# Half of an MLP's up projections by seven half-size products in place of eight, on one Trainium2 core

## The chip, the cores and the metric

The kernel runs on one core of one Trainium2 chip. The core has a matrix engine (TensorE, PE in the profile; its weight loads are PEld), a vector engine (VectorE, DVE), a scalar engine (ScalarE, ACT), GpSimd (POOL) and SyncE (SP), whose queue issues nearly all DMA transfers here. The metric is the device time of one execution in microseconds, as the median of several runs.

## The reference

The program is a decoder trunk of two layers over 256 tokens of width 2048, in float32. Layer 0 uses differential attention, layer 1 latent attention; each layer then attends into 256 memory tokens and ends in a squared-ReLU MLP with 8192 hidden columns.

```python
def sq_relu_mlp(h, wup, wdown):
    return jnp.square(jax.nn.relu(h @ wup)) @ wdown

def reference(...):
    mem_h = rms_norm(mem, mem_norm)
    for i in range(DEPTH):                   
        h = rms_norm(x, attn_norm[i])
        x = x + (diff_attention if i % 2 == 0 else mla_attention)(h, ...)
        x = x + memory_cross_attention(rms_norm(x, cross_norm[i]), mem_h, ...)
        x = x + sq_relu_mlp(rms_norm(x, mlp_norm[i]), mlp_wup[i], mlp_wdown[i])
    return rms_norm(x, final_norm)
```

wup is 2048 x 8192, wdown 8192 x 2048. The MLP is the largest part: two products of 256 x 2048 x 8192 in each layer.

## The kernel before

**Arithmetic.** Every product of float32 matrices is made of three TensorE passes. Each operand is split into a high part (a cast to the matrix format) and a low part (the rest), and high x high, high x low and low x high are added up in PSUM.

**Weights.** A weight matrix is stored as units of 512 rows of K by 512 columns, 1 MB each, laid out as 128 partitions x 2048. `split_weights` (L173) loads one into a `raw` buffer (4 of them, `RAWS`), and for each half of it ScalarE casts the high part `whi` (L187) and VectorE subtracts to get `wlo` (L188). `whi` and `wlo` have four half-size buffers each (`whalf`), so TensorE's halves of the current unit and the next one fill them. `plan` is the list of all units in order of use; `fill` (L195) keeps `AHEAD` = 3 of them issued ahead, and `take` (L203) hands over the next one. Loads stand in program order on SP's queue.

**Matmuls.** `matmul_chunk` (L212) makes 256 x 512 outputs in two PSUM banks, one per tile of 128 tokens (t = 0, 1). A unit of weights gives 2 halves x 2 token tiles x 2 pieces of K x 3 passes = 24 matmuls of 128x128 by 128x512. All matmuls are recorded at L155, all transposes (128x128, also on TensorE) at L159.

**Order.** TensorE's instructions run in the order in which the program writes them. The other engines' order is set by a scheduler at build time. To place transposes among matmuls, the program keeps a clock of its own (`clock`): work that follows a chunk is a `Task`, a generator that yields how many microseconds its next step should be put off, and `pump` (L113), called after every part of a unit, runs the steps that are due. `need` (L120) forces the tasks that a matmul depends on. The constants `T_SQ` = 4.4, `T_TURN` = 2.6, `T_ADD` = 2.2 are such put-offs. Nothing checks them against the chip: where a step is placed too early, TensorE stands until its input is there.

**The MLP** (`mlp`, L808) has four blocks of 2048 hidden columns. `up` (L813) makes four chunks of 512 columns, each from 4 units; per token tile, ScalarE takes relu and the row's scale out of PSUM (L821), GpSimd squares (L822), TensorE transposes four times, and `split` (L268) makes the high and low parts of the hidden columns as the stationary operand of the next product. `down` makes four chunks of the output from the block's four hidden tiles and adds each to the residual rows `x` (L349). The order is up 0, down 0, up 1, and so on.

**Around it.** `Stream.feed` (L329) turns the residual rows after the last projection into the transposed, split operand of the next layer part. PSUM has eight banks, four for matmul chunks (`ps_mm`) and four for everything else (`ps_ax`). The attention parts use tiles `ev`, `xg`, `p` and `pT` of the pool `work`; `mem_norm` (L719) loads the memory rows into `xg` tiles; `tables` (L686) makes the rotary tables, from constants and positions that are loaded by hooks at the first six units.

Of the kernel before, what the change touches and what calls it, by code (L numbers as in the profile page):

```python
# [23 lines left out]
WARM = 16  # L24
RAWS = 4
MLP_BLOCKS = 4

# [16 lines left out]
def trunk(ctx, tc, x, xT, mem, memT, positions, gcols, gfinal, lam_vecs, consts, W, out):  # L44
# [24 lines left out]
    def half_unit():  # L69
        return units.tile([P, 2, 2, S], F32R, tag="half", name=nm("half"), bufs=3)  # L70

    def bank(tag="ax"):
        p = ps_mm if tag == "mm" else ps_ax
        return p.tile([P, CH], F32, tag=tag, name=nm(tag))

# [51 lines left out]
    class Held:  # L127
# [6 lines left out]
        def run(self, gen):  # L134
            self.tasks.append(Task(gen))
            return self

        def __getitem__(self, i):
            return self.tile[i]
# [21 lines left out]
    def f32(ap):  # L161
        return ap.bitcast(F32)
# [10 lines left out]
    def split_weights(src, width, pieces=2, loads=1, queue=None):  # L173
        raw = raw_tile()
        n = 4 * width
        m = n // loads
        for i in range(loads):
            load(raw[:, i * m : (i + 1) * m], src[:, i * m : (i + 1) * m], queue)
        m = n // pieces
        halves = []  # L180
        for i in range(pieces):
            at = i * m % (n // 2)
            if at == 0:
                halves.append([whalf.tile([P, 2 * CH], F32R, tag=tag, name=nm(tag)) for tag in ("whi", "wlo")])
            hi, lo = (w[:, at : at + m] for w in halves[-1])
            r = raw[:, i * m : (i + 1) * m]
            nc.scalar.copy(hi, r)  # L187
            nc.vector.tensor_tensor(lo, r, f32(hi), ALU.subtract)  # L188
        return halves

    plan = []
    ready = []
    AHEAD = 3

    def fill():  # L195
        while len(ready) < AHEAD and plan:
            name, i, width = plan.pop(0)
            ready.append(split_weights(W[name][i, :, : 4 * width], width))

# [3 lines left out]
    def take():  # L203
# [6 lines left out]
        return got  # L210

    def matmul_chunk(acts, width=CH, turns=False):  # L212

# [3 lines left out]
        def part(u, h, hi, lo, t):  # L217
            o = ps[t][:, :width]
            a = acts[u]
            for k in range(2):  # L220
                kk = 2 * h + k
                first = u == 0 and kk == 0
                last = u == n - 1 and kk == 3
                ah = a[:, 0, kk, t * P : (t + 1) * P]
                al = a[:, 1, kk, t * P : (t + 1) * P]
                wh = hi[:, k * width : (k + 1) * width]
                wl = lo[:, k * width : (k + 1) * width]
                mmul(o, ah, wh, first, False)
                mmul(o, ah, wl, False, False)
                mmul(o, al, wh, False, last)  # L230
            pump()

# [22 lines left out]

    const = keep.tile([P, NC_], F32, name="const")
    g = keep.tile([P, NG], F32, name="g")
    pos = keep.tile([P, NT], I32, name="pos")
    lamv = work.tile([P, 4, P], F32, tag="ev", name="lamv", bufs=6)
    xs = [keep.tile([P, D], F32, name=f"x{t}") for t in range(NT)]  # L260
    ident = const[:, C_ID : C_ID + P]
    identr = keep.tile([P, P], F32R, name="identr")
    maskr = keep.tile([P, P], F32R, name="maskr")
    mhalf = keep.tile([P, 1], F32, name="mhalf")
# [10 lines left out]
    def scaled(src, cols):  # L275
        tmp = work.tile([P, 4, P], F32, tag="xg", name=nm("xg"))
        nc.vector.tensor_tensor(tmp, src, cols.unsqueeze(2).broadcast_to([P, 4, P]), ALU.mult)  # L277
        return tmp
# [42 lines left out]
    class Stream:  # L321


        def __init__(self, gcol):
            self.gcol = gcol
            self.units = {}
            self.ss = [small.tile([P, 4], F32, tag="ss", name=nm("ss")) for _ in range(NT)]

# [14 lines left out]
        def done(self):  # L343
            self.rstd = [row_norm(self.ss[t], D)[:, 0:1] for t in range(NT)]
            return [self.units[c] for c in range(4)]

    def add_residual(t, c, ps):
        xc = xs[t][:, c * CH : (c + 1) * CH]
        nc.vector.tensor_tensor(xc, xc, ps, ALU.add)  # L349


    def evacuate(ps, scale):
        e = work.tile([P, CH], F32, tag="ev", name=nm("ev"), bufs=6)
        nc.scalar.activation(e[:, : ps.shape[1]], ps, AF.Copy, scale=scale)  # L354
        return e
# [47 lines left out]
    def softmax(sb, n):  # L403
# [3 lines left out]
        ssum = small.tile([P, 4], F32, tag="ssum", name=nm("ssum"))  # L407
        pr = work.tile([P, CH], F32, tag="p", name=nm("p"), bufs=3)
        nc.vector.tensor_reduce(nmax[:, :n], sb.rearrange("p (n k) -> p n k", n=n), AX.X, ALU.max, negate=True)  # L409
# [9 lines left out]
    def prob_T(src, n, pt):  # L419

        for i in range(n):
            flip(pt[:, i * P : (i + 1) * P], src[:, i * P : (i + 1) * P])
        o = work.tile([P, 2, CH], F32R, tag="pT", name=nm("pT"), padded_shape=[P, 2, 4 * S])
# [102 lines left out]
    def attend_diff(q, k, v, dst, coef, subcols):  # L526
# [33 lines left out]
        def normed(t, blocks, out):  # L560
# [6 lines left out]
            r = rsqrt_mean(ss, 2, S)  # L567
            os = work.tile([P, CH], F32, tag="p", name=nm("os"), bufs=3)
            nc.vector.tensor_tensor(
# [43 lines left out]
    def plan_mlp(l):  # L613
        for b in range(MLP_BLOCKS):
            plan_k(f"mlp_wup{l}", 16, start=16 * b)
            plan_k(f"mlp_wdown{l}", 16, start=16 * b)

# [68 lines left out]
    def tables():  # L686
# [26 lines left out]
        for i in range(2):  # L713
            nc.vector.tensor_scalar(gsub[:, 2 * i : 2 * i + 2], g[:, G_SUB : G_SUB + 2], 1.0 - LAMBDA_INIT, None, ALU.mult)
        nc.scalar.copy(identr, ident)
        nc.scalar.copy(maskr, const[:, C_MASK : C_MASK + P])
    mem_rstd = []

    def mem_norm():  # L719
        for t in range(NT):  # L720
            ss = small.tile([P, 4], F32, tag="ss", name=nm("ss"))
            for c in range(4):
                mt = work.tile([P, CH], F32, tag="xg", name=nm("memrow"), padded_shape=[P, 4 * P])
# [29 lines left out]
    def project_out(acts_o, gcol):  # L753
        nxt = Stream(gcol)
        for c in range(4):
# [52 lines left out]
    def mlp(l, norm, gnext):  # L808
# [3 lines left out]

        def up(b):  # L813
            hid[b] = []
            for c in range(4):
                dst = Held(unit())
                ps = matmul_chunk(a)

                def task(t, ps, dst):
                    r = work.tile([P, CH], F32, tag="ev", name=nm("ev"), bufs=6)  # L820
                    nc.scalar.activation(r, ps, AF.Relu, scale=rstd[t])  # L821
                    nc.gpsimd.tensor_tensor(r, r, r, ALU.mult)  # L822
                    yield T_SQ
                    split(dst, t, transpose4(r, ps))
                    yield T_TURN

                for t in range(NT):
                    dst.run(task(t, ps[t], dst))
                hid[b].append(dst)

        def down(b, nxt=None):
            for c in range(4):
                ps = matmul_chunk(hid[b], turns=nxt is not None and c == 3)
                for t in range(NT):
                    add_residual(t, c, ps[t])
                    if nxt is not None:
                        nxt(c, t, ps[t])

        for b in range(MLP_BLOCKS):
            up(b)  # L840
            if b < MLP_BLOCKS - 1:
                down(b)
        if gnext is None:
            return down
        nxt = Stream(gnext)
        down(b, nxt.feed)
        return nxt

# [37 lines left out]
    hm = MLA_ROPE // 2  # L886
    krope = Held(half_unit())
    LAT = 3 * P
# [23 lines left out]
    def latent_rows():  # L912
        return [work.tile([P, CH], F32, tag="ev", name=nm("lat"), bufs=6) for _ in range(NT)]

# [11 lines left out]
    for t in range(NT):  # L926
        e = work.tile([P, 2, P], F32, tag="kr", name=nm("kr"))
        nc.vector.memset(e, 0.0)
# [72 lines left out]
    load(gf, gfinal)  # L1001
    ss = [small.tile([P, 4], F32, tag="ss", name=nm("ss")) for _ in range(NT)]

# [17 lines left out]

    down(MLP_BLOCKS - 1, finish)

# [86 lines left out]
```

## Time and profile before

| what | value |
|---|---|
| median of 3 runs | 2323.3 us (2322.37 to 2324.17) |
| profiled execution, its own time | 2322.5 us |
| span of its instructions | 2320.8 us |
| mean granted TensorE clock | 0.997 |
| MLP of layer 0 / layer 1, about | 543 to 1230 us / 1629 to 2310 us |
| DMA | 425.36 MB, 183 GB/s over the span |
| matmuls at L155, mean recorded duration | 9504 of chunks, 387 to 389 ns (neighbours overlap) |
| one 1 MB weight load, issue to landing | 5.0 us |
| GpSimd's square (L822), x64 | 1272 ns |
| ScalarE's relu (L821), x64 | 685 ns |

Matmuls overlap in the records, so their rate is read from a stretch: its length by the number of matmuls in it. An "idle before" column says how long an engine stood ahead of a group, and behind the arrow what ended it.

### The profile page before, as it was taken

The page shows a single profiled execution, that of the slowest core. Times are in us where ns is not written, and L with a number is a line of the kernel's source. Part 1 is how long each engine was busy: PE and PEld are TensorE (multiplying, and loading weights), DVE is VectorE, ACT ScalarE, POOL GpSimd, SP SyncE. Part 2 cuts the span into 40 slices and gives each one's busy share as a digit, 9 for nine tenths or more (in the row PEclk, how much of TensorE's full clock was granted, in tenths as well). Part 3 has the DMA queues.
Part 4 walks back from the last instruction along what each step waited for, and adds up shares of the span by engine and source line. Part 5 has one row for each costly group of instructions (what it writes and reads, how often), then busy time and mean ns, then how long its engine had stood idle before and what let it go on. Part 6 is the DMA issues. An engine that isn't in the chain of part 4 may idle for free.

```text
span 2320.8 us, 27365 instructions
## 1 busy us (share of the span) xinstructions
PE 2295.0 (99%) x10860; PEld 1920.4 (83%) x10860; DVE 1300.9 (56%) x1502; ACT 1131.7 (49%) x1539; POOL 188.5 (8%) x258
## 2 busy tenths in 40 slices
PE   8999999999999999999999999999999999999998
PEld 6888888888888888888889888888888888888886
DVE  5555647674554554454455766777454454445454
ACT  6544545664434434434454655555443443443443
POOL 0111110000000000000000311000100100100101
PEclk9999999999999999999999999999999999999999
DMA  8455555545555555555555444544555555555563
GB/s 316 145 176 171 198 184 197 182 145 184 193 188 193 186 194 187 184 197 188 187 174 178 145 143 157 200 164 164 181 190 192 190 189 190 191 183 198 182 207 119
DMA packets 65217, 425.36 MB, mean 183 GB/s; under 512 B 7488, under 2 KB 7616, under 8 KB 16448
## 3 DMA queue, kind: packets, MB, share of 16 engines
q1 hardware_dynamic: 64512, 422.56, 53.3%
q8 instruction: 85, 1.39, 0.2%
q10 hardware_dynamic: 576, 1.05, 0.2%
q14 instruction: 44, 0.36, 0.0%
HBM read 421.48 MB, written 2.10 MB: 183 GB/s over the span
## 4 chain that ended last, share of the span: by engine, by line
PE 95%; DVE 1%; DMA 1%; ACT 1%; POOL 1%; issue 1%; ACTq 0%; SPq 0%; POOLq 0%
PE mm L155 89%; PE ax L155 2%; PE mm L159 2%; PE ax L159 1%; DVE wlo L188 1%; DMA memrow<-in_mem_dram 1%; DMA raw<-in_da_wqkv_dram 0%; ACT whi L187 0%; ACT junk L301 0%; POOL rope L367 0%; DVE x L349 0%; DVE nmax L409 0%; POOL ev L369 0%; POOL rope L366 0%; DVE unit L398 0%
## 5 line engine op out<-in xcount | busy, mean ns | idle before, releaser
L155 PE MATMUL mm<-whi,unit 128*128 128x512 f32 (+2 forms) x6336 | 1971.0, 389 | 2.6 <-ACT unit L294 1.6
L188 DVE TENSOR_TENSOR wlo<-raw,whi 128x1024 fp32r<-128x1024 f32 (+2 forms) x794 | 962.8, 1213 | 928.3 <-ACT whi L187 927.2
L155 PEld LDWEIGHTS mm<-whi,unit 128*128 128x128 f32 x6336 | 1186.0, 188 | 239.2 <-ACT unit L294 2.1
L187 ACT CAST whi<-raw 128x1024 fp32r<-128x1024 f32 (+2 forms) x794 | 826.6, 1041 | 1048.8 <-PE mm L155 1028.0
L155 PE MATMUL mm<-wlo,unit 128*128 128x512 f32 (+2 forms) x3168 | 1224.6, 387 | 0.8 <-DVE wlo L188 0.8
L155 PEld LDWEIGHTS mm<-wlo,unit 128*128 128x128 f32 x3168 | 595.7, 188 | 115.2 <-DVE wlo L188 1.3
L822 POOL TENSOR_TENSOR ev<-ev 128x512 f32<-128x512 f32 x64 | 81.4, 1272 | 1160.3 <-ACT ev L821 1159.1
L349 DVE TENSOR_TENSOR x<-x,mm 128x512 f32<-128x512 f32 x144 | 94.9, 681 | 9.9 <-PE mm L155 9.2
L307 POOL TENSOR_TENSOR rs<-rs,mhalf 128x1 f32<-128x1 f32 (+1 forms) x28 | 21.4, 770 | 673.8 <-DVE rs L306 638.2
L273 DVE TENSOR_TENSOR unit<-mm,unit 128x512 fp32r<-128x512 f32 x88 | 56.6, 684 | 5.2 <-ACT unit L272 4.5
L159 PE MATMUL mm<-const,ev 128*128 128x128 f32 x352 | 46.8, 276 | 6.1 <-POOL ev L370 6.1
L159 PEld LDWEIGHTS mm<-const,ev 128*128 128x128 f32 x352 | 41.6, 142 | 12.5 <-POOL ev L370 6.9
L272 ACT CAST unit<-mm 128x512 fp32r<-128x512 f32 x88 | 47.2, 586 | 8.8 <-PE mm L159 8.8
L821 ACT ACTIVATE ev<-mm,r 128x512 f32<-128x512 f32 x64 | 43.8, 685 | 11.6 <-PE mm L155 11.6
L411 ACT ACTIVATE p<-ax,nmax 128x256 f32<-128x256 f32 (+1 forms) x80 | 33.6, 428 | 22.9 <-DVE nmax L409 22.5
L301 ACT ACTIVATE junk<-x 128x512 bf16<-128x512 f32 x56 | 35.2, 629 | 15.1 <-DVE x L349 13.0
L272 ACT CAST unit<-xg 128x512 fp32r<-128x512 f32 x52 | 31.9, 623 | 15.3 <-DVE xg L277 12.7
L273 DVE TENSOR_TENSOR unit<-xg,unit 128x512 fp32r<-128x512 f32 x52 | 35.7, 696 | 3.0 <-ACT unit L272 2.8
L155 PE MATMUL ax<-unit,unit 128*128 128x256 f32 (+1 forms) x240 | 37.2, 281 | 0.0
L155 PEld LDWEIGHTS ax<-unit,unit 128*128 128x128 f32 x240 | 34.3, 190 | 2.5
L365 POOL TENSOR_TENSOR rope<-ev,cos 128x64 f32<-128x64 f32 (+1 forms) x24 | 14.2, 593 | 226.2 <-ACT ev L354 226.0
L277 DVE TENSOR_TENSOR xg<-mm,g 128x512 f32<-128x512 f32 x40 | 26.1, 686 | 10.2 <-PE mm L159 10.2
(121 smaller groups left out, 613.7 us busy)
## 6 DMA issues: line engine op xcount, KB each, us to landing
raw<-in_mlp_wup_dram SPq DMA_DIRECT2D x128, 1024.0 KB, 5.0
raw<-in_mlp_wdown_dram SPq DMA_DIRECT2D x128, 1024.0 KB, 5.0
raw<-in_da_wqkv_dram SPq DMA_DIRECT2D x47, 1024.0 KB, 5.0
raw<-in_da_wo_dram SPq DMA_DIRECT2D x16, 1024.0 KB, 4.9
raw<-in_ca_wkv_dram SPq DMA_DIRECT2D x16, 1024.0 KB, 5.0
raw<-in_mla_wo_dram SPq DMA_DIRECT2D x16, 1024.0 KB, 5.1
raw<-in_ca_wq_dram SPq DMA_DIRECT2D x8, 1024.0 KB, 5.0
raw<-in_ca_wo_dram SPq DMA_DIRECT2D x8, 1024.0 KB, 4.9
```

What stands on the lines that cost most here:

```text
L155: return nc.tensor.matmul(o, stationary, moving, start=start, stop=stop)
L159: nc.tensor.transpose(o, src, ident)
L187: nc.scalar.copy(hi, r)
L188: nc.vector.tensor_tensor(lo, r, f32(hi), ALU.subtract)
L272: nc.scalar.copy(hi, src)
L273: nc.vector.tensor_tensor(dst[:, 1, :n, t * P : (t + 1) * P], src, f32(hi), ALU.subtract)
L277: nc.vector.tensor_tensor(tmp, src, cols.unsqueeze(2).broadcast_to([P, 4, P]), ALU.mult)
L301: nc.scalar.activation(junk[:, : src.shape[1]], src, AF.Square, accum_out=acc)
L349: nc.vector.tensor_tensor(xc, xc, ps, ALU.add)
L411: nc.scalar.activation(pr[:, i * w : (i + 1) * w], sb[:, i * w : (i + 1) * w], AF.Exp, bias=nmax[:, i : i + 1], accum_out=ssum[:, i : i + 1],)
L821: nc.scalar.activation(r, ps, AF.Relu, scale=rstd[t])
L822: nc.gpsimd.tensor_tensor(r, r, r, ALU.mult)
```

## The change

The MLP is cut into eight blocks of 1024 hidden columns. In blocks 1, 3, 5 and 7 the up projection is done as a 2 x 2 product of blocks: the activations A are cut into token tiles and halves of K (A11, A12, A21, A22), the weights B into halves of K and chunks of 512 columns. Seven products of 128 x 1024 by 1024 x 512 (p1 to p7), of sums and differences of these, give the four outputs of 128 x 512 that eight products gave. One item of a product (p, x) is one combined weight unit, x being the half of its K, and gives 12 matmuls.

- The class `Forms` replaces `Stream` ahead of the MLP. It keeps A in a layout by token tile, keeps the raw transposed rows in two raw buffers, and makes s1 to s4 (sums and differences) with high and low parts.
- The class `Seven` loads the raw weights, combines them on VectorE in place (128 x 2048), splits the result as before, and adds the products up from PSUM on VectorE into `ev` tiles; then relu, square and four transposes per output.
- `mlp_line` writes the order: items of the seven products are dealt out among the ordinary items of the surrounding `down` and `up`. `down` runs over one or two waiting blocks at a time.
- Squares are an activation of ScalarE in place of a product on GpSimd.
- Buffers: 6 raw buffers, 4 units ahead, 12 activation units, one pool of eight PSUM banks, `ev` takes over `xg` and `p` with 7 buffers, `small` has 3 in place of 6, and the attentions' `pT` tiles and the shared rotary key live in raw buffers.

```diff
-RAWS = 4
-MLP_BLOCKS = 4
+RAWS = 6
+MLP_BLOCKS = 8
+SEVEN = (1, 3, 5, 7)
+EVS = 7
...
-    units = pool("units", 10)
+    units = pool("units", 12)
...
-    small = pool("small", 6)
-    ps_mm = pool("ps_mm", 4, bass.MemoryType.PSUM)
-    ps_ax = pool("ps_ax", 4, bass.MemoryType.PSUM)
+    small = pool("small", 3)
+    banks = pool("banks", 8, bass.MemoryType.PSUM)
...
-    AHEAD = 3
+    AHEAD = 4
...
+    class Forms(Stream):
...
+        def sums(self):
...
+            for x in range(2):
+                a11, a12, a21, a22 = (self.raw[t][:, 8 * h + 4 * x : 8 * h + 4 * x + 4] for t in range(NT) for h in range(2))
+                for key, o, p, q, op in (
+                    ("s1", a22, a21, a22, ALU.add), ("s3", a21, a11, a21, ALU.subtract),
+                    ("s2", a22, a22, a11, ALU.subtract), ("s4", a12, a12, a22, ALU.subtract),
+                ):
+                    nc.vector.tensor_tensor(o, p, q, op)
+                    self.halves(key, x, o)
+                yield T_TURN
...
-        pTs = [work.tile([P, 2, 2, 2, S], F32R, tag="pT", name=nm("pT")) for _ in range(2)]
+        pTs = [raw_tile().bitcast(F32R).rearrange("p (a b c d) -> p a b c d", a=2, b=2, c=2) for _ in range(2)]
...
+    class Seven:
...
+        ORDER = ("p1", "p5"), ("p3", "p7", "p6", "p2", "p4")
+        A = {"p1": (0, 0), "p2": (0, 1), "p3": "s4", "p4": (1, 1), "p5": "s1", "p6": "s2", "p7": "s3"}
...
+        def job(self, p, x):
+            def run():
+                r = self.raw
+                if p == "p1":
+                    r["11"] = o = self.fetch(0, 0, x)
+                elif p == "p5":
+                    o = self.fetch(0, 1, x)
+                    nc.vector.tensor_tensor(o, o, r.pop("11"), ALU.subtract)
+                elif p == "p3":
+                    r["22"] = o = self.fetch(1, 1, x)
+                elif p == "p7":
+                    r["t3"] = o = self.fetch(0, 1, x)
+                    nc.vector.tensor_tensor(o, r.pop("22"), o, ALU.subtract)
+                elif p == "p6":
+                    r["t2"] = o = self.fetch(0, 0, x)
+                    nc.vector.tensor_tensor(o, r.pop("t3"), o, ALU.add)
+                elif p == "p2":
+                    r["21"] = o = self.fetch(1, 0, x)
+                else:
+                    o = r.pop("t2")
+                    nc.vector.tensor_tensor(o, o, r.pop("21"), ALU.subtract)
+                return halves_of(o)
...
+        def products(self, a, u, copied, out):
...
+            for h, (hi, lo) in enumerate(take()):
+                for k in range(2):
+                    kk = 4 * x + 2 * h + k
+                    wh, wl = (w[:, k * CH : (k + 1) * CH] for w in (hi, lo))
+                    mmul(o, form[:, 0, kk], wh, kk == 0, False)
+                    mmul(o, form[:, 0, kk], wl, False, False)
+                    mmul(o, form[:, 1, kk], wh, False, kk == 7)
+                pump()
...
+            if p in ("p1", "p5"):
+                c[p] = work.tile([P, CH], F32, tag="ev", name=nm(p), bufs=EVS)
+                nc.scalar.copy(c[p], o)
+            elif p == "p6":
+                u2, c12 = (work.tile([P, CH], F32, tag="ev", name=nm("u"), bufs=EVS) for _ in range(2))
+                add(u2, b["p6"], c["p1"])
+                add(c["p5"], u2, c["p5"])
+                add(c12, b["p3"], c["p5"])
+                out(0, 1, c12)
+                add(c["p5"], b["p7"], c["p5"])
+                out(1, 1, c["p5"])
+                add(u2, b["p7"], u2)
+                c["u3"] = u2
+            elif p == "p2":
+                add(c["p1"], b["p2"], c["p1"])
+                out(0, 0, c["p1"])
+            elif p == "p4":
+                add(c["u3"], c["u3"], b["p4"], ALU.subtract)
+                out(1, 0, c["u3"])
+
+    def mlp_line(l):
...
+        line = up(0)
+        waiting = [0]
+        for b in SEVEN:
+            rest = down(waiting) + (up(b + 1) if b < 7 else [])
+            seven = Seven(l, b).items()
+            i = 0
+            for k, item in enumerate(rest):
+                while i < len(seven) and i * (len(rest) - 3) / len(seven) <= k:
+                    line.append(seven[i])
+                    i += 1
+                line.append(item)
+            waiting = [b, b + 1] if b < 7 else [b]
+        return line + down(waiting)
...
+            def task():
+                nc.scalar.activation(r, src, AF.Relu, scale=rstd[t])
+                nc.scalar.activation(r, r, AF.Square)
+                yield wait
+                pt = yield from side_bank()
+                split(dst, t, transpose4(r, pt))
+                yield T_TURN
+                give_back()
```

For the products `wait` is T_SQ + 2.0 = 6.4, for ordinary chunks T_SQ. Within the MLP one side bank at a time may be in use for transposes (`limit`).

More of the change, by code (lines that the diff above doesn't have):

```diff
@@ L69, in half_unit @@
     def half_unit():
-        return units.tile([P, 2, 2, S], F32R, tag="half", name=nm("half"), bufs=3)
+        return units.tile([P, 2, 2, S], F32R, tag="half", name=nm("half"), bufs=2)
     def bank(tag="ax"):
-        p = ps_mm if tag == "mm" else ps_ax
-        return p.tile([P, CH], F32, tag=tag, name=nm(tag))
+        return banks.tile([P, CH], F32, tag="bank", name=nm(tag))
     clock = [0.0]
@@ L136, in run, with get @@
             return self
+        def get(self, half, kk, t):
+            return self.tile[:, half, kk, t * P : (t + 1) * P]
         def __getitem__(self, i):
@@ L217, in part @@
         def part(u, h, hi, lo, t):
[L218 to L231, printed above, removed]
+            unit_part(ps[t][:, :width], acts[u], h, hi, lo, t, u == 0, u == n - 1)
         def ready_unit(u):
@@ L347, in add_residual, with __init__, get @@
+    class FormUnit:
+        def __init__(self, forms, u):
+            self.tiles = [forms.form((t, u // 2)) for t in range(NT)]
+            self.at = 4 * (u % 2)
+            self.tasks = [k for f in self.tiles for k in f.tasks]
+        def get(self, half, kk, t):
+            return self.tiles[t][:, half, self.at + kk]
     def add_residual(t, c, ps):
@@ L613, in plan_mlp, with __init__, items @@
     def plan_mlp(l):
-        for b in range(MLP_BLOCKS):
-            plan_k(f"mlp_wup{l}", 16, start=16 * b)
-            plan_k(f"mlp_wdown{l}", 16, start=16 * b)
+        plan.extend(j for item in mlp_lines[l] for j in item.jobs)
+    class Chunk:
+        def __init__(self, l, kind, blocks, c):
+            self.kind, self.blocks, self.c = kind, blocks, c
+            if kind == "up":
+                self.all = [(f"mlp_wup{l}", 4 * (2 * blocks[0] + c) + u, CH) for u in range(4)]
+            else:
+                self.all = [(f"mlp_wdown{l}", 8 * b + 2 * c + u, CH) for b in blocks for u in range(2)]
+        def items(self):
+            return [Item(self, u, [job]) for u, job in enumerate(self.all)]
@@ new lines, in mlp_line, with up, down @@
+    def mlp_line(l):
+        def up(b):
+            return [i for c in range(2) for i in Chunk(l, "up", [b], c).items()]
+        def down(blocks):
+            return [i for c in range(4) for i in Chunk(l, "down", blocks, c).items()]
+        line = up(0)
[11 more added lines that the diff above has]
+        return line + down(waiting)
@@ L618, in trunk @@
+    mlp_lines = {l: mlp_line(l) for l in range(2)}
     plan_cross(0)
@@ L811, in mlp @@
         hid = {}
[L813 to L835, printed above, removed]
-                    if nxt is not None:
[L837 to L842, printed above, removed]
+        chunk = {}
+        copied = {}
+        def out(b, c, t, src, r, wait):
+            if (b, c) not in hid:
+                hid[b, c] = Held(unit())
+            dst = hid[b, c]
+            def task():
+                nc.scalar.activation(r, src, AF.Relu, scale=rstd[t])
[3 more added lines that the diff above has]
+                split(dst, t, transpose4(r, pt))
+                yield T_TURN
+                give_back()
+            dst.run(task())
@@ new lines, in finish_chunk, with acts_of @@
+        def finish_chunk(of, ps, nxt):
+            for t in range(NT):
+                if of.kind == "up":
+                    r = work.tile([P, CH], F32, tag="ev", name=nm("ev"), bufs=EVS)
+                    out(of.blocks[0], of.c, t, ps[t], r, T_SQ)
+                else:
+                    add_residual(t, of.c, ps[t])
+                    if nxt is not None:
+                        nxt(of.c, t, ps[t])
+        def acts_of(of):
+            if of.kind == "up":
+                return [a.unit_of(u) for u in range(4)]
+            return [hid[b, c] for b in of.blocks for c in range(2)]
@@ new lines, in run @@
+        def run(line, nxt=None):
+            for item in line:
+                of = item.of
+                if isinstance(of, Seven):
+                    of.products(
+                        a, item.u, copied,
+                        lambda t, c, r, b=of.b: out(b, c, t, r, r, T_SQ + 2.0),
+                    )
+                    continue
+                n = len(of.all)
+                if nxt is not None and of.c == 3:
+                    if item.u == 0:
+                        finish_chunk(of, matmul_chunk(acts_of(of), turns=True), nxt)
+                    continue
+                if item.u == 0:
+                    chunk["ps"] = [bank("mm") for _ in range(NT)]
+                    chunk["acts"] = acts_of(of)
+                act = chunk["acts"][item.u]
+                need(act.tasks)
+                for h, (hi, lo) in enumerate(take()):
+                    for t in range(NT):
+                        unit_part(chunk["ps"][t], act, h, hi, lo, t, item.u == 0, item.u == n - 1)
+                if item.u == n - 1:
+                    finish_chunk(of, chunk["ps"], nxt)
@@ L843, in mlp, with last @@
+        line = mlp_lines[l]
+        tail = sum(len(i.of.all) == 2 and i.of.kind == "down" and i.of.blocks == [7] for i in line if not isinstance(i.of, Seven))
+        limit = free_banks[0] - 1
+        free_banks[0] -= limit
+        run(line[:-tail])
+        def last(nxt):
+            free_banks[0] += limit
+            run(line[-tail:], nxt)
         if gnext is None:
-            return down
+            return last
         nxt = Stream(gnext)
-        down(b, nxt.feed)
+        last(nxt.feed)
```

117 lines of the change are left out of this document (97 added, 20 removed).

## The prediction

> **What bounds the kernel now.** I read the busy times first, then TensorE's own waits, then the chain of waits inside one MLP, then VectorE's timeline there, then stretches of clock and DMA.
>
> ```profile
> span 2320.8 us, 27365 instructions
> ...
> PE 2295.0 (99%) x10860; PEld 1920.4 (83%) x10860; DVE 1300.9 (56%) x1502; ACT 1131.7 (49%) x1539; POOL 188.5 (8%) x258
> ...
> L188 DVE TENSOR_TENSOR wlo<-raw,whi 128x1024 fp32r<-128x1024 f32 (+2 forms) x794 | 962.8, 1213 | 928.3 <-ACT whi L187 927.2
> ...
> L187 ACT CAST whi<-raw 128x1024 fp32r<-128x1024 f32 (+2 forms) x794 | 826.6, 1041 | 1048.8 <-PE mm L155 1028.0
> ```
>
> TensorE (PE) is busy for 99% of the span. VectorE (DVE) and ScalarE (ACT) idle about half of it: ScalarE's cast waits for TensorE to free a half of the weights, and VectorE's subtraction waits for the cast. From 437 us on, TensorE waited this much in all:
>
> ```profile
> PE ax L159 <- POOL ev L370: 1.0, 1, 1.0
> PE mm L155 <- ACT unit L482: 0.9, 2, 0.4
> PE ax L155 <- ACT unit L397: 0.6, 2, 0.3
> PE ax L159 <- DVE pT L465: 0.5, 1, 0.5
> ```
>
> That is 3 us, none of it in either MLP. The chain from 540 to 800 us is matmuls and transposes alone:
>
> ```profile
> 610.50 108.84 PE mm L155 x480
> 719.34 0.88 PE mm L159 x8
> 720.22 21.80 PE mm L155 x96
> ```
>
> So the MLP lasts as long as its matmuls: 108.84 / 480 = 0.2268 us each. Whatever removes a matmul there shortens the kernel, provided that the rest still keeps up.
>
> **What is removed.** An ordinary block of 1024 hidden columns is 2 chunks x 4 weight units x 24 matmuls = 192. The seven products are 7 x 2 items of 12 matmuls (4 pieces of K, 3 passes each, one token tile) = 168. So 24 go per block; blocks 1, 3, 5, 7 of both layers make 8 x 24 = 192, and 192 x 0.2268 = **43.5 us off the path**. The transposes stay: 16 chunks of 512 columns x 8 per layer before and after. [...] The chain shows 226.8 ns, and I use that.
>
> **What feeds it, in the tight stretch (block 1).** There 14 product items alternate with 16 ordinary ones (8 of down, 8 of up). TensorE: 168 x 0.2268 + 16 x 5.44 + 32 transposes x 0.11 = 128.7 us. VectorE:
> - splitting: 30 items x 2 x 1.213 = 72.8.
> - combining raw weights, p5, p7, p6, p4, each twice: eight 128x2048 subtractions or additions. The trace has none. 128x512 takes 0.684 (L273), 128x1024 takes 1.213, so 0.53 per 512 more; twice 1.213 is a ceiling (2.43), the slope gives 1.213 + 2 x 0.53 = 2.27. I take 2.3: 18.4.
> - adding products from PSUM: 7 x 0.69 (L349's 0.681) = 4.8.
> - the rest: 8 residual adds x 0.681 = 5.4, 8 splits of hidden rows x 0.684 = 5.5.
>
> Sum 106.9, or 83% of TensorE's 128.7. Block 7 has 16 down items instead: about 104 of 127. Blocks 3 and 5 have 24 ordinary items: about 127 of 172. ScalarE in block 1 has 60 casts x 1.041 = 62.5, and 8 x (0.685 relu + 0.63 square + 0.586 cast) + 2 copies = 16.5: 79 us, 61%. Both fit on average.
>
> The worst pair, one combining product and one ordinary item, costs VectorE 4 x 1.213 + 2.3 + 0.68 = 7.8 against TensorE's 12 x 0.2268 + 5.44 = 8.16 us. It fits only because splits run ahead: four half-item buffers (whalf) allow a product's half to be split in the 6.8 us between the end of the half that used the buffer and its own start, and an ordinary half in 5.4 us, against cast 1.04 + subtract 1.21. VectorE's row shows this reserve today:
>
> ```profile
> 774.86 1.23 DVE L188 TENSOR_TENSOR wlo<-raw,whi 128x1024 fp32r<-128x1024 f32 x1 [1.49 <-ACT whi L187]
> 777.58 1.22 DVE L188 TENSOR_TENSOR wlo<-raw,whi 128x1024 fp32r<-128x1024 f32 x1 [1.49 <-ACT whi L187]
> ```
>
> Each subtraction starts 1.5 us after the last ended. A 2.3 us combination pushes the next by under 1 us, which the 3 to 4 us of reserve hold. Price 0 while that cover stands; without it see the second case.
>
> **Squares to ScalarE.** 64 x 1.27 leave GpSimd, 64 x 0.63 (the form of L301, already the same function) come to ScalarE, which is 61% busy at most there. The page's groups have three table loads in all, though L301 alternates with copies and relu throughout, so no reload. Off the path: 0.
>
> **DMA.** Each product block fetches 12 units, not 8: 32 more of 1.05 MB in all. Block 1 moves 28 units in 129 us, 228 GB/s. The start shows more is to be had:
>
> ```profile
> 30.00:40.00 10.00, 10.00 (x46) 8.28 (x45) 5.34 (x8) 7.95 (x16) 0.56 (x1) 1.00 1.03 405
> ```
>
> One landing takes 5.0 us. Of six raw buffers the products keep up to two back (p7's and p6's for later combinations) besides one in use, so three loads lead by 3 x 4.08 = 12 us. Hidden: 0; if the lead fell below 5 us it would be the transfer that lands last.
>
> **Transposes of the products' results: the new wait.** TensorE's order is fixed in program order. After p6's last item, u2, c5 and c12 are formed one after another on VectorE, then relu and square on ScalarE: 3 x 0.69 + 0.69 + 0.63 + some 0.4 of hand-over = 3.8 us. The planner puts the transposes 6.4 us behind (T_SQ + 2.0). So VectorE may be behind by 2.6 us before TensorE stands; at that moment it can hold one subtraction (1.2) and one combination (2.3), 3.5 us. Behind the waiting transpose stand all later matmuls; what is late next is nothing else, as splits then get ahead. Bounds per block: 0 and, with another combination and a cast in front, 3 us. I take 0.75, as mostly only the first of the four results comes in a burst: 8 x 0.75 = **+6** (0 to 24).
>
> **Banks.** With p3, p7, p6, p2, p4 open, three of eight banks remain. In blocks 3 and 5 the last down chunk is followed at once by an up chunk whose second bank waits for a residual add: needed 1.36 us after the chunk's end, free after 0.9 to 3.2. Four such places, 0 to 1.8 us: **+2** (0 to 7).
>
> **Start and attention.** Four items are queued ahead instead of three, so one more 1 MB load (2.6 us at 400 GB/s) stands on SP's queue before constants, positions and rows of x; the stall before 55 us (5.4 us on POOL ev L370) may grow by it, and six buffers may shorten the early waits: -2 to +3, I take **+1**. In attention, probabilities now take two of the six raw buffers, and the shared key one: three for weights where four were. With three, a load goes out when the unit three before is split, 2.4 us after the start of the unit four before; it lands by 7.4 and is split from 13.6 (2.5 units of 5.44), so 0 (0 to 20: third case). The memory rows' eight loads get seven buffers for two; today they hold SP's queue 15 us at 242 us and no TensorE wait follows: 0. The Forms' 16 additions and 16 casts with subtractions per layer lie under 43 us of up(0), where VectorE idles half: 0. The added residual adds, 2 x 8 x 0.68, go into the same idle time: 0.
>
> **Sum**, against the profiled execution (2322.5 us, span 2320.8): 2322.5 - 43.5 + 6 + 2 + 1 = 2288.0. The runs' median, 2323.3, lies 0.8 higher, so 2288.8, **2289 us**. Its own range is 2279 to 2297.
>
> **Rivals.**
> - *VectorE binds in the tight pairs.* If each of the four subtractions of a pair loses 0.3 us between hand-overs, 7.8 becomes 9.0 against 8.16: 0.84 lost at 8 combining pairs in 4 tight blocks, 27 us in the place of my 8: 2308. For it: the subtract idles until its cast today. Against: pairs that combine nothing have 2.5 us to catch up.
> - *Attention pays for the shared buffers.* Eight head groups and two cross attentions wait 2 us each: +20, 2309. For it: DVE is 70% busy there (158.2 of 224 us, 1300 to 1524). Against: the lead worked out above.
> - *Slower: every result comes late.* If VectorE holds the product additions behind splits and combinations that were queued earlier, all 32 sets of transposes stand 2.5 us each: 80 instead of 6, 2363. It decides from 1.36 us per set (43.5 / 32). For it: additions follow in program order behind loads four items ahead. Against: the residual adds in the MLP today end within 1.3 us of each other with no TensorE wait.
>
> Long stalls cost twice, as the start shows (the granted clock is the number ahead of the DMA share):
>
> ```profile
> 48.00:55.00 7.00, 1.15 (x5) 0.75 (x5) 2.55 (x9) 3.88 (x6) 3.53 (x12) 0.76 0.57 207
> 55.00:57.00 2.00, 2.00 (x7) 1.81 (x8) 0.91 (x2) 0.59 (x1) 0.00 (x0) 0.50 0.00 0
> ```
>
> TensorE stood most of 7 us and then had half the clock: 66 matmuls from 56.1 us took 16.2 us instead of 15.0, so 1.2 lost again. The rows can't tell whether 2.5 us of standing would do it; if so, the last case costs 32 x 1.2 = 38 more, 2401. [...]
>
> **Chances.** Forecast 0.63, tight pairs 0.15, attention 0.08, late results 0.14. This kernel's measurement tells 0.2% (4.6 us) from no change. The late results at a price near 1.36 us, and the tight pairs at their worst, give 0.03 within that; faster 0.85, slower 0.12. The range goes from 2277 (no wait at all, a start 2 us better) to 2314 (both middle cases and a little more); the late results beyond it are left out.
>
> **What would show it.** Matmuls of 128x512 fewer by 192, still 227 ns apart; VectorE up by about 330 us to some 70% of the span; TensorE's waits after 437 us between 5 and 15 us, at transposes released by ScalarE's square and at matmuls released by residual adds. Wrong if waits on wlo appear (second case), waits in the attention stretches (third), or the clock drops inside an MLP (fourth).

## The result, and the profile after

The changed kernel takes **2285.2 us** (median of 4 runs, 2284.5 to 2286.2) against 2323.7 before; the ratio is 0.9835, with a 95% interval of 0.9818 to 0.9852. The forecast was 2289 in a range of 2277 to 2314. The profiled execution has a span of 2282.7 us, 38.1 less than the one before.

The page of the changed kernel, busy times and the groups that answer to those shown before, and as a fifth line one of the four lines of the pass that combines raw weights:

```profile
span 2282.7 us, 27403 instructions
...
PE 2255.7 (99%) x10668; PEld 1884.4 (83%) x10668; DVE 1609.0 (70%) x1766; ACT 1281.1 (56%) x1731; POOL 103.4 (5%) x194
...
L194 DVE TENSOR_TENSOR wlo<-raw,whi 128x1024 fp32r<-128x1024 f32 (+2 forms) x890 | 1071.6, 1212 | 560.1 <-ACT whi L193 541.1
L193 ACT CAST whi<-raw 128x1024 fp32r<-128x1024 f32 (+2 forms) x890 | 926.1, 1041 | 850.8 <-PE mm L158 763.2
...
L748 DVE TENSOR_TENSOR raw<-raw,raw 128x2048 f32<-128x2048 f32 x16 | 36.7, 2292 | 0.5
```

TensorE has 192 matmuls fewer (10860 to 10668) and is still busy for 99%. VectorE rose by 308 us, and TensorE hardly waits for it. Of its waits over the whole span, these three lines matter (in all, times, longest):

```profile
PE mm L162 <- POOL ev L449: 7.6, 2, 7.0
PE ax L162 <- POOL ev L449: 2.1, 1, 2.1
...
PE ax L162 <- ACT u L1027: 1.3, 2, 0.7
```

The first is the stall near 50 us, 6.1 before; the second lies in the latent attention, 1.0 before; only the third, one wait of 0.7 us in block 1 of each layer, lies in the MLPs. The chain of waits inside the first MLP, pr being the seven products and L162 transposes:

```profile
559.28 2.72 PE pr L158 x12
562.00 2.72 PE mm L158 x12
564.73 0.44 PE ax L162 x4
565.16 2.77 PE mm L158 x12
```

Matmuls of product items and ordinary ones run at the old rate, 0.2267 us each (2.72 / 12). Starts of the same stretches in both chains of waits give an account of the 38.1 us (the row of 108 matmuls at the end of the cross attention, that of 192 at the start of the latent attention):

| stretch | before | after | difference | by the count of matmuls |
|---|---|---|---|---|
| start to the first MLP | 517.13 | 517.47 | +0.34 | 0 |
| MLP of layer 0, to 1232.00 / 1212.40 | 714.87 | 694.93 | -19.94 | -21.77 |
| layer 1 before its MLP, to 1603.75 / 1585.35 | 371.75 | 372.95 | +1.20 | 0 |
| MLP of layer 1 and the end | 717.05 | 697.35 | -19.70 | -21.77 |

Each MLP gave back about 2 us. Of these 0.7 is the wait. About 1 is the transposes: before, eight stood together, now two sets of four. The matmuls behind a set start late by about 0.05 us (12 in 2.77 instead of 2.72 above), and there are 32 sets in a layer in place of 16; 16 more sets make 0.8 us.

### The profile page after: what moved, and what is told of

Its sections match the earlier page's. It is cut to its first block, busy times and chain, and to the rows that moved or that the text cites. A ratio compares the mean times of both kernels' runs of the same rounds, so it can differ in the third digit from the quotient of the medians.

```text
span 2282.7 us, 27403 instructions
## 1 busy us (share of the span) xinstructions
PE 2255.7 (99%) x10668; PEld 1884.4 (83%) x10668; DVE 1609.0 (70%) x1766; ACT 1281.1 (56%) x1731; POOL 103.4 (5%) x194
## 4 chain that ended last, share of the span: by engine, by line
PE 96%; ACT 1%; DVE 1%; DMA 1%; POOL 0%; issue 0%; ACTq 0%; POOLq 0%; SPq 0%
PE mm L158 77%; PE pr L158 13%; PE ax L158 3%; PE ax L162 2%; PE mm L162 1%; ACT whi L193 1%; DMA raw<-in_da_wqkv_dram 0%; DVE wlo L194 0%; DMA raw<-in_memT_dram 0%; POOL rope L444 0%; POOL ev L449 0%; ACT junk L311 0%; ACT ev L433 0%; ACT p L490 0%; POOL rope L447 0%
## 5 line engine op out<-in xcount | busy, mean ns | idle before, releaser
L158 PE MATMUL mm<-whi,unit 128*128 128x512 f32 (+1 forms) x5312 | 1679.7, 389 | 1.4 <-ACT unit L561 0.9
L194 DVE TENSOR_TENSOR wlo<-raw,whi 128x1024 fp32r<-128x1024 f32 (+2 forms) x890 | 1071.6, 1212 | 560.1 <-ACT whi L193 541.1
L193 ACT CAST whi<-raw 128x1024 fp32r<-128x1024 f32 (+2 forms) x890 | 926.1, 1041 | 850.8 <-PE mm L158 763.2
L158 PEld LDWEIGHTS mm<-whi,unit 128*128 128x128 f32 x5312 | 994.5, 188 | 198.2 <-ACT unit L561 1.3
L158 PE MATMUL mm<-wlo,unit 128*128 128x512 f32 (+1 forms) x2656 | 1026.1, 386 | 0.8 <-DVE wlo L194 0.8
L158 PEld LDWEIGHTS mm<-wlo,unit 128*128 128x128 f32 x2656 | 500.3, 188 | 95.6 <-DVE wlo L194 1.4
L158 PE MATMUL pr<-whi,unit 128*128 128x512 f32 x896 | 298.0, 391 | 0.0
L158 PEld LDWEIGHTS pr<-whi,unit 128*128 128x128 f32 x896 | 168.3, 188 | 34.6
L158 PE MATMUL pr<-wlo,unit 128*128 128x512 f32 x448 | 174.4, 389 | 0.0
L743 DVE TENSOR_TENSOR raw<-raw,raw 128x2048 f32<-128x2048 f32 x16 | 36.6, 2290 | 10.0 <-DMA raw<-in_mlp_wup_dram 9.8
L735 DVE TENSOR_TENSOR raw<-raw,raw 128x2048 f32<-128x2048 f32 x16 | 36.6, 2286 | 3.3 <-DMA raw<-in_mlp_wup_dram 2.6
L740 DVE TENSOR_TENSOR raw<-raw,raw 128x2048 f32<-128x2048 f32 x16 | 36.6, 2288 | 3.2 <-DMA raw<-in_mlp_wup_dram 3.0
L748 DVE TENSOR_TENSOR raw<-raw,raw 128x2048 f32<-128x2048 f32 x16 | 36.7, 2292 | 0.5
```

Of the source, the lines that this page charges most:

```text
L158: return nc.tensor.matmul(o, stationary, moving, start=start, stop=stop)
L735: nc.vector.tensor_tensor(o, o, r.pop("11"), ALU.subtract)
L740: nc.vector.tensor_tensor(o, r.pop("22"), o, ALU.subtract)
L743: nc.vector.tensor_tensor(o, r.pop("t3"), o, ALU.add)
L748: nc.vector.tensor_tensor(o, o, r.pop("21"), ALU.subtract)
```

## The experiments

Theory: the matmuls count in full, because VectorE, ScalarE and the loads keep ahead; what is lost are transposes placed too early. Rivals: VectorE binds in the tight pairs; late results cost more than is gained; other edits bring the gain or take it.

**No products (no_seven).** Alone undone: the seven products.

```diff
-        line = up(0)
-        waiting = [0]
-        for b in SEVEN:
...
-        return line + down(waiting)
+        line = []
+        for b in (0, 2, 4, 6):
+            line += up(b) + up(b + 1)
+            if b < 6:
+                line += down([b, b + 1])
+        return line + down([6]) + down([7])
```

> All eight blocks of the MLP go up by ordinary chunks (192 matmuls each); buffers, eight blocks, squares on ScalarE and the single side bank stay. s1 to s4 are formed but not used. If the whole gain is the 192 matmuls, this is the changed kernel plus 43.5 us less its two waits of 0.7 us: 2327 us, within 3. If the other edits bring part of the gain, or if the products lose much of it again in waits, it is clearly lower: 2300 to 2315.

Measured: 2327.0 us (ratio to before 1.0012, 1.0003 to 1.0021). The products are worth 41.9 us, as 43.5 less two waits says, and all other edits together cost 3.5 us. The sets of four and the latent attention (its wait of 2.1 us is there without products too) are part of it; how the rest divides is not shown, for two executions took 2324.3 and 2324.4 us at a mean clock of 0.998, the other eight 2326.5 to 2327.4 at 0.996. Taken together these edits gain nothing; of single ones, only the squares and the raw buffers were tried.

**More work for VectorE (comb2, comb3).** One or two further passes after each combination.

```diff
+                if p in ("p5", "p7", "p6", "p4"):
+                    for _ in range(1):
+                        nc.vector.tensor_tensor(o, o, o, ALU.max)
                 return halves_of(o)
```

(2 in place of 1 for comb3.)

> Each combination of raw weights on VectorE is followed by one more pass of the same size over the same buffer (maximum of it with itself, 2.29 us, 64 in all, +147 us of VectorE). If VectorE has the reserve that the count of block 1 says (107 of 129 us, now 125 of 129), TensorE loses 0 to 15 us: 2285 to 2300. If the tight pairs bind already, each extra pass in the tight blocks is paid in full: 8 x 4 x 2.29 = 73 us, 2358.

> Two more passes per combination. By the count, block 1 now needs 143 us of VectorE against 129 of TensorE and block 7 141 against 127, blocks 3 and 5 164 against 172: 2 x (14 + 14) = 56 us more, 2341 (2330 to 2360). If the tight pairs bound already, 2 x 73 = 147: 2432. If VectorE does not matter at all, 2285.

Measured: comb2 2319.5 us, comb3 2388.8 us. Neither reading of comb2 fits: 34 us lie between 15 and 73. TensorE's waits in comb2 name the place, and there is hardly one for a weight (wlo):

```profile
PE ax L162 <- ACT u L1030: 22.7, 8, 4.1
...
PE mm L158 <- DVE wlo L194: 1.0, 2, 0.8
```

Eight waits, the first transposes of each block's results: 4.1 us in block 1 and 2.4 in the others. So VectorE fed the weights in time, and the results came late behind the extra passes. The 22.7 us of waits don't make 34; most of the rest is the clock, 0.992 on the mean against 0.996, some 9 us of 2300. Stretches around one of the waits (the granted clock is the number ahead of the DMA share):

```profile
1000.00:1003.00 3.00, 3.00 (x15) 2.50 (x14) 3.00 (x4) 1.34 (x2) 0.00 (x0) 1.00 0.95 352
1003.00:1006.00 3.00, 0.98 (x5) 0.47 (x3) 2.63 (x4) 2.67 (x4) 0.00 (x0) 1.00 0.86 320
1006.00:1008.00 2.00, 1.60 (x8) 1.38 (x9) 1.30 (x2) 1.97 (x4) 0.00 (x0) 0.82 0.84 262
1008.00:1010.00 2.00, 2.00 (x7) 1.54 (x6) 1.34 (x2) 0.74 (x2) 0.00 (x0) 0.50 0.59 246
```

TensorE stands 2.4 us before 1006.4 and then runs at half clock, its matmuls 0.43 us apart from 1008.26 on in place of 0.227. In comb3 the same eight waits reach 54.5 us, up to 10.0 each, and now weights and hidden rows are late too:

```profile
PE ax L162 <- ACT u L1030: 54.5, 8, 10.0
PE mm L158 <- DVE wlo L194: 8.2, 12, 1.7
...
PE mm L158 <- DVE unit L283: 5.2, 2, 2.6
PE pr L158 <- DVE wlo L194: 3.5, 2, 2.0
```

That agrees with VectorE at its bound, as the count of 143 against 129 us has it. The time rose by 103.6 us and not by 56: the four kinds of waits make 71, and the matmuls that ran at half clock behind them lost about 24 us more than in the changed kernel (mean clock 0.981 against 0.996, but a part of the half clock fell into the stops themselves and cost nothing). Some 10 us are not accounted for.

**Is that VectorE, or the place of the transposes? (comb2_w84)**

```diff
-                        lambda t, c, r, b=of.b: out(b, c, t, r, r, T_SQ + 2.0),
+                        lambda t, c, r, b=of.b: out(b, c, t, r, r, T_SQ + 4.0),
```

> comb2 (one more pass per combination, 2319 us) with the transposes 2.0 us further back. comb2 stood eight times at the first result of a block, 2.4 to 4.1 us, 22.7 in all, and the clock fell behind some of them. If late results are its whole cost, 2.0 us less of each leave 8 x 0.4 + 2 x 1.7 = 7 us and no drop of the clock: 2292. If VectorE itself is the bound with the extra passes, the wait goes elsewhere and the time stays: 2315 to 2320.

Measured: 2296.8 us, 22.7 less than comb2 with the same work on every engine. The eight waits shrink to 7.8 us in all (longest 2.3). So VectorE with 125 of 129 us of work still feeds the matmuls; two thirds of the 34 us of comb2 were an order written too tightly. Of the 11.5 us that are left above the changed kernel, 6.5 are waits for results.

**The place itself (wait24, wait84).** The same line with T_SQ - 2.0 and T_SQ + 4.0, on the changed kernel.

> The transposes of the products' results are placed 2.4 us behind the product in TensorE's order instead of 6.4. In the changed kernel the first result of block 3 is ready 5.5 us after p6's end and that of block 1 7.4 us. If these transposes hold TensorE until the result is there, at least the first of each block costs 2.8 us (22 us in all, 2307), and all four up to 8 us (64, 2349). If the put-off hardly matters, 2285.

> The transposes of the products' results are placed 8.4 us behind the product instead of 6.4. The changed kernel stood twice, 0.7 us each in block 1, where the result was ready 7.4 us after the product against a place at 6.8. If that is all that late results cost, both waits go and the time falls by 1.4 us, to 2284; nothing else moves. If the put-off has a price of its own (hidden columns late for the down projection), the time rises: 2287 or more.

Measured: wait24 2329.8 us, 44.6 more than the changed kernel, which loses the whole gain (ratio to before 1.0025, 1.0014 to 1.0036). It lies between the two forecasts: the first result of each block costs 2.8 us, as expected, and six of the later ones 1.7. Its waits:

```profile
PE ax L162 <- ACT u L1027: 23.1, 10, 2.8
PE ax L162 <- ACT p L1027: 10.0, 6, 1.7
```

33 us are waits, most of the rest again half clock: behind the start seven stretches of 3.41 us, where the changed kernel's profile has one, make 10 us (half of each is taken as lost, 1.7 us, an estimate from the clock of 0.50). wait84 took 2286.0 us, no less than the changed kernel: in its profile the 1.3 us of waits at squares are gone, as expected, but in that execution the start is later, with 66 matmuls behind the first stall in 17.4 us instead of 16.5, and a stop of 2.06 us in the latent attention, which the changed kernel has too, is followed here by 3.41 us of half clock, which costs 1.7. 1.4 us can't be told from such spread, so on the time this run is inconclusive.

**Loads (raws5).** `RAWS = 5` in place of 6.

> Five raw buffers instead of six, all else as in the changed kernel (2285). With up to two held by the products and one in use, two loads lead by 2 x 4.08 = 8 us, against 5.0 us for a landing: no wait in the MLP; in the latent attention two are left for weights beside the probabilities and the shared key, which may cost a few us: 2285 to 2292. If raw buffers limit the products, TensorE waits on casts that wait on loads in the MLP: 2295 or more.

Measured: 2290.0 us. The same account as above, by stretches:

| stretch | changed kernel | raws5 |
|---|---|---|
| start to the first MLP | 517.47 | 519.88 |
| MLP of layer 0 | 694.93 | 695.10 |
| layer 1 before its MLP | 372.95 | 375.60 |
| layer 1's MLP, to the row of 234 matmuls | 635.39 | 635.30 |

In both MLPs a buffer less costs nothing, so the loads have lead to spare there, although they move 227 GB/s in block 1. All of it is lost ahead of the MLPs, where the attentions' probabilities and the shared key hold raw buffers. Longer waits make about 1.0 us of layer 1's 2.65; the other 1.7 are half clock behind the same stop of 2.06 us as in wait84, so not all of the 4.8 us is shown to be a matter of buffers.

**Squares back on GpSimd (pool_sq).**

```diff
-                nc.scalar.activation(r, r, AF.Square)
+                nc.gpsimd.tensor_tensor(r, r, r, ALU.mult)
```

> Squares back on GpSimd, all else as in the changed kernel. If squares lie off TensorE's path, only the two places in block 1 that are late already get later, by the 0.64 us between 1.27 and 0.63 and some queueing: 2285 to 2288. If GpSimd and VectorE hinder each other, wlo's mean of 1212 ns grows and more results are late: 2290 or more.

Measured: 2285.9 us, the same as the changed kernel. One square takes 1.37 to 1.55 us there and wlo grows from 1212 to 1222 ns, and neither shows in the time. The two late places did not get later, as expected, but shrank from 1.3 to 0.8 us in all. Moving the squares bought nothing and cost nothing that can be told.

**The stall at the start (pub8, pub8_w84).** Not part of the change, but the longest wait left: transposes of the first rotary projection, placed before its tables are done.

```diff
     hooks[6] = first_norm
+    hooks[8] = lambda: published.append(True)
+    published = []
...
-                    given=lambda: da_scales,
+                    given=lambda: published,
```

> The scales of the first projection are made known to the program's clock two units later (at the eighth unit instead of the sixth), so the first rotary transposes stand about 11 us later in TensorE's order; loads, tables and everything else stay. If the 7.0 us for which TensorE stands near 50 us is a place too early in its order, the stall and the half clock behind it (1 us) go: 2277. If the stall only moves to the next transposes or into the first attention, 2285.

> Both shifts of transposes together: first rotary transposes two units later, products' results at 8.4 us. pub8 measured 2275.7 and has the two waits of 0.7 us in block 1 left: 2274.3. If the put-off of 8.4 us has a price elsewhere: 2276 or more.

Measured: 2275.7 us for pub8, 9.5 less than the changed kernel, for an edit that only holds these transposes, and the reading of their chunks out of PSUM that goes with them, back by two units. The shorter stall makes 5.8 us; in the profiles the rest is half clock, which behind the start's 74 us is gone too (the changed kernel has 3.41 us of it at 378 us). What is left of the wait, and the first 74 us of it (clock 1.00, where the changed kernel has 0.93):

```profile
PE mm L162 <- POOL ev L449: 1.8, 2, 1.1
```

```profile
0.00:74.00 74.00, 70.07 (x301) 54.07 (x302) 43.88 (x77) 46.52 (x76) 10.56 (x30) 1.00 0.83 318
```

pub8_w84 took 2276.4 us: as with wait84, the further 2 us of put-off make no difference that this measurement tells.

**Five blocks (five).** On pub8_w84, blocks 1, 3, 4, 6 and 7 by seven products.

```diff
+        first = up(0)
+        line = first[:4]
+        for b, rest in (
+            (1, first[4:] + down([0])),
+            (3, down([1]) + up(2)),
+            (4, down([2, 3])),
+            (6, down([4]) + up(5)),
+            (7, down([5, 6])),
+        ):
```

> pub8_w84 with five of eight blocks by seven products (1, 3, 4, 6, 7), each dealt among 12 to 16 ordinary items, the first among the second half of up 0 and down 0. Another 2 x 24 matmuls go, 10.9 us: 2263.4, if VectorE keeps up; by the count it needs about 107 of 129 us in four of the five and 101 to 114 of 107 in the first, so up to 7 us may be lost there in each layer: 2264 to 2277. If VectorE's reserve is used up with four blocks, the time stays at 2274 or rises.

Measured: **2268.0 us** (ratio to before 0.9761, 0.9746 to 0.9775), the fastest of all. 8.5 of the 10.9 us arrive, with VectorE at 74%. The profiled execution, the slowest of four, has two stretches of half clock in the attentions that pub8_w84's does not have, which cost 3.3 us, and TensorE waits 2.5 us for wlo against 1.4; so the missing 2.4 us are not shown to be VectorE's:

```profile
PE 2244.8 (99%) x10620; PEld 1874.4 (83%) x10620; DVE 1684.2 (74%) x1836; ACT 1306.5 (58%) x1759; POOL 106.1 (5%) x194
```

## Why the prediction was right, point by point

**What bounds the kernel, and the 43.5 us.** Right. The products run at the ordinary rate, and taking them away alone costs 41.9 us. Of the prediction's signs, VectorE's 70% came true (308 us more, 330 forecast), and TensorE's waits after 437 us are 5.5 us, at the low end of 5 to 15; only 1.3 of them are at squares, the rest in the attentions, and none is at a residual add.

**VectorE in the tight stretch.** The count was 106.9 of 128.7 us. The stretch of block 1, VectorE being the third busy time:

```profile
559.00:691.00 132.00, 131.34 (x596) 108.45 (x595) 103.98 (x92) 79.02 (x90) 0.00 (x0) 1.00 0.65 227
```

104 of 132, ScalarE's 79.0 as counted. A combination takes 2.29 us (2.3 was worked out). The price 0 for the feed stands: even with one more pass each, almost no matmul waited for a weight. The second case, tight pairs that bind, is refuted for this kernel by comb2_w84: with twice the combining work TensorE waits 1.6 us in all for wlo, 0.8 in the changed kernel. In the runs it comes true only at three times the combining work. The zeros for squares and loads stand as well, by pool_sq and by the MLP rows of raws5.

**Late results.** The mechanism is right, the term was too large: 6 us forecast, 1.3 measured. Block 1's chain, first on VectorE, then on ScalarE; p6 ends at 652.73:

```profile
653.64 0.68 DVE L775 TENSOR_TENSOR u<-pr,p 128x512 f32<-128x512 f32 x1
654.24 1.22 DVE L194 TENSOR_TENSOR wlo<-raw,whi 128x1024 fp32r<-128x1024 f32 x1
655.37 0.68 DVE L775 TENSOR_TENSOR p<-u,p 128x512 f32<-128x512 f32 x1
656.09 0.69 DVE L775 TENSOR_TENSOR u<-pr,p 128x512 f32<-128x512 f32 x1
```

```profile
656.85 0.69 ACT L1026 ACTIVATE ev<-mm,r 128x512 f32<-128x512 f32 x1 [0.30 <-PE mm L158]
657.43 0.71 ACT L1026 ACTIVATE u<-u,r 128x512 f32<-128x512 f32 x1
658.05 0.62 ACT L1027 ACTIVATE ev<-ev 128x512 f32<-128x512 f32 x1
658.57 1.03 ACT L193 CAST whi<-raw 128x1024 fp32r<-128x1024 f32 x1
659.51 0.62 ACT L1027 ACTIVATE u<-u 128x512 f32<-128x512 f32 x1
```

On VectorE one split came between, not the combination and a split together, as the bound had it: c12 (the last u) was ready 4 us after p6. Then ScalarE, which the 3.8 us of the prediction took as free (only its upper bound has a cast in front), had an ordinary chunk's relu, its square and a cast in turn with it, because that chunk ends at the same moment in block 1. The result was ready 7.4 us after p6, against a place at 6.8. In block 3 nothing crosses it on ScalarE; ready after 5.5, no wait. The last case, late results that eat up the gain, is what wait24 shows, and comb2 in large part. It was near: in block 3 the first result had 1.3 us to spare.

**Banks, start, attention.** Banks: 2 forecast, no wait found, the residual add came in time. Start: +1 forecast, +0.34, a net of both of its terms: the stall on GpSimd grew from 6.1 to 7.6 us, while two waits of before, 1.6 us for the first operands and 1.5 us on a cast, shrank to 0.5 and went. Attention: 0 forecast, +1.2, nearly all of it one rotary transpose that now waits 2.1 us for GpSimd instead of 1.0. Why its rotation is later stays open: it waits as long in no_seven, so the products are not the cause, and raws5 shows only that the attentions are where raw buffers are short. **Not in the sum:** the sets of four transposes, about 2 us for both layers; the prediction counted the transposes, which stayed, and not the changes between them and matmuls.

So -43.5 + 1.4 (waits) + 2.5 (what is left of both MLPs, mostly the sets of four) + 0.3 + 1.2 = -38.1, where the forecast had -34.5. The large term was right for the reason given. That the sum is only 3.6 us off is in part luck: waits, banks and start were put 7.3 us too high, the attention and the sets of four 3.7 too low. The third case, the attention at +20 us, came true in direction only.

## What to carry to other kernels

Where one engine is at 99% and its work is a count of equal instructions, the saving is count times rate (here 192 x 0.2268 = 43.5 us, of which 41.9 were measured in no_seven), and the question is only whether the others keep ahead. Test that by adding work to the engine in doubt, and look at which instruction then waits: here it was never the feed first, but results whose consumer had a fixed place in the order of the bound engine. In such an order, work that has to come back from another engine should be placed with more room than its mean needs: here a place 2 us later cost nothing that could be measured (wait84), and one 4 us earlier cost 44.6 us (wait24).

## What the runs showed of the hardware that was not expected

The half clock came behind shorter stops than the 7 us at the start that the prediction had seen, and not each time. TensorE's idle times ahead of transposes in comb2 and wait24, and the granted clock over the 4 us behind each:

| idle before | times | clock fell to 0.57 to 0.70 | clock stayed 1.00 | largest empty share of one 3.41 us window (see below): where it fell / where it stayed |
|---|---|---|---|---|
| 1.67 us | 6 | 0 | 6 | - / 0.30 to 0.49 |
| 1.75 us | 2 | 1 | 1 | 0.67 / 0.38 |
| 2.06 us | 2 | 2 | 0 | 0.60 / - |
| 2.42 us | 6 | 2 | 4 | 0.59 and 0.71 / 0.36 to 0.48 |
| 2.80 us | 8 | 6 | 2 | 0.60 to 0.82 / 0.46 and 0.57 |
| 4.1 us | 2 | 2 | 0 | 0.84 and 1.00 / - |

The last column goes with what the clock did. Up to the last matmul, the stretches at a granted clock of 0.50 last 6.83 us before, and 10.24 and 3.41 us in the changed kernel: twice, three times and once 3.413 us. In the changed kernel they start at 49.99 and 377.67 us, 96 x 3.413 apart; in wait24 four of them start at 824.00, 1001.50, 1148.27 and 1295.04 us: 52, 43 and 43 times. For the column, each profile's time was therefore cut into windows of 3.413 us at its own marks. In the whole profiles of before and of the changed kernel, in both MLPs of comb2 (540 to 1245 and 1600 to 2305 us) and in wait24 from 1785 to 2305 us, a window at full clock in which TensorE's matmul and transpose records leave 59 to 100% empty was followed by half clock 8 times in 8 (1, 1, 4 and 2); with 57% or less that happened once (50%, in the changed kernel at 374 us) in some 1880 windows. Stops of equal length so differed in effect: behind those of 2.42 us in comb2 the clock fell where 59 and 71% of one window were empty, and stayed at 36 to 48%. The stop of 2.06 us in the latent attention was followed by half clock in comb2, wait24, wait84 and raws5, and not in the changed kernel, where 41% of a window was empty.

The prediction left open whether 2.5 us of standing would do what 7 us did. Stops of 2.42 us did it 2 times in 6, those of 2.80 us 6 times in 8. So its price behind each late result, 1.2 us, came true for part of them. In comb2's stretch behind 1006.4 us matmuls start 0.43 us apart, so 3.41 us hold 8 of them in place of 15, and 1.6 us are lost beside the stop, close to the 1.7 us estimated above.
